# A decoder layer whose input norm moves behind the first matmuls

## The chip, the core and the metric

The kernel runs on one core of a Trainium2 chip. The core has a matmul engine (PE, with its weight loads PEld), three engines for elementwise work (DVE, ACT, POOL), a queue engine (SP) that issues most transfers, and 16 DMA engines. The metric is the device time of one execution in microseconds (us). The kernel before takes 607.66 us, the median of three runs that lie between 607.46 and 608.18.

## The reference, cut to what matters

One layer of a hybrid decoder on 1024 tokens of 1024 features, in float32. `D = S = 1024`; there are four heads of differential attention (group A) and four of chunkwise retention (group B), each with 128 columns of values.

```python
u = rmsnorm(h, norm_pre_w)                     # h * rsqrt(mean(h*h) + eps) * w, per token
proj = einsum('bsd,de->bse', u, w_in)          # 1024 x 1024 @ 1024 x 4096
dq, dk, dv, dg, rq, rk, rv, rg = split(proj)   # 512 columns each
lam = exp(sum(q1*k1)) - exp(sum(q2*k2)) + lambda_init
# group A: rotary on dq, dk; p_c = softmax(causal(q_c k_c^T / 8)), c = 0, 1; (p_0 - lam * p_1) @ dv
y_a = rmsnorm(diff_attention(dq, dk, dv, positions, lam), diff_subln_w) * (1 - lambda_init)
y_a = y_a * silu(dg)
# group B: rotary on rq, rk; scores decayed by g^(i-j), g = 1 - 2^-(5+head), times rv
y_b = rmsnorm(retention_chunkwise(rq, rk, rv, positions)) * silu(rg)
y = concatenate([y_a, y_b]) @ w_out
return h + rmsnorm(y, norm_post_w)
```

The factor 1/rms of the first line belongs to one token, so it is the same for all of a token's features. A projection of the unnormalised token, times that factor, is the projection of the normalised one.

## The kernel before

**Tiles.** Tokens stand in `NT = 8` tiles of 128, features in `KT = 8` tiles of 128. `u` is held transposed (features on the partitions), in halves of 512 tokens, each as two parts that add up to the float32 value: `uh` (rounded to the format that the matmul multiplies) and `ul` (the rest). `w_in` comes as 16 packed blocks of 256 columns, in the order of `ORDER`: part 0 of a head holds its values and gates, part 1 its queries and keys. A block is loaded in four chunks (`load_chunk`, L147), each rounded by ACT into `whi` and completed by DVE or POOL in turn into `wlo` (`split_lo`, L141; two of four turns each). A product is three matmuls: `uh*whi + uh*wlo + ul*whi` (L296 to L298 for outputs with tokens on the partitions, L308 to L310 for transposed outputs).

**The beginning.** For each token tile, `norm_tile` (L257) squares x on ACT with a running sum, takes `(mean + eps) ** -0.5` with DVE and POOL (`rsqrt`, L132), multiplies x by it and by the gain on DVE (L272), transposes the eight 128x128 pieces on PE into two PSUM banks (L278), and splits them into `uh` (ACT, L281) and `ul` (DVE, L282). After every second tile, `main_group(0, ...)` multiplies two token tiles by block 0 (`proj_rows`, L285) into one of two PSUM banks named `pj`. Then come the angles of the rotary embedding (`angles`, L174: a long chain on DVE, two sines on ACT, 16 transposes on PE at L229) and the rest of the blocks.

**The rest.** `main_group(b, g)` is a quarter of a block. What the quarter yields is read from PSUM by `values_gates` (L313: values by ACT at L321 or L325, `tanh` of the gate by ACT at L327, `gt = (tanh + 1) * gate` by DVE at L328), by `diff_qk` (L354, with the rotary factors `cosD`, `sinD`) or by `ret_qk` (L458, with `cosE`, `sinE`). Between the quarters stand pieces of other heads' attention and retention. The last block's quarters are followed by the output projection.

**What sets the order.** The program is written once, in one stream. A scheduler then puts each engine's instructions in a fixed order by its own estimate of when each can run; so PE's queue interleaves pieces that stand apart in the code, and SP's queue holds loads ahead of those that the code writes first. On the chip each engine takes its queue strictly in that order.

Of the kernel before, what the change touches and what calls it, by code (L numbers as in the profile page):

```python
# [10 lines left out]
F32 = mybir.dt.float32  # L11
# [20 lines left out]
# Column layout of the constants that depend on shapes alone.  # L32
# [8 lines left out]
# Heads (differential 0-3, retention 4-7) and the order of their blocks of w_in:  # L41
# part 0 holds the values and gates, part 1 the queries and keys.
# [46 lines left out]
def body(ctx, tc, x, pos, wpk, wout, vecs, npre, npost, subln, cst, out):  # L89
# [32 lines left out]
    cs = const.tile([P, NCST], F32, name="cs")  # L122
# [6 lines left out]
    halves = const.tile([P, 2], F32, name="halves")  # L129
    nc.gpsimd.memset(halves, -0.5)  # L130

    def rsqrt(dst, src, more):  # L132
        """(src + more) ** -0.5"""
# [7 lines left out]
    def split_lo(dst, full, hi):  # L141
        """dst = full - hi, rounded to the tensor engine's operand (exact)."""
# [31 lines left out]
    def angles(tp, posi):  # L174
        """cos and sin of position * frequency, with an exact reduction to one turn."""
# [29 lines left out]
        # small parts first  # L205
# [8 lines left out]
        # cos x = sin(x + a quarter turn)  # L214
# [32 lines left out]
    def load_x(xin, t):  # L247
        xt = xin.tile([P, D], F32, tag="xt", name="xt")
        rows = slice(t * P, (t + 1) * P)
        if t == 0:  # L250
            nc.sync.dma_start(xt[:, 0:512], x[rows, 0:512])
            nc.scalar.dma_start(xt[:, 512:], x[rows, 512:])
        else:
            nc.sync.dma_start(xt, x[rows, :])
        return xt

    def norm_tile(xp, t, xt, npw):  # L257
        xu = xp.tile([P, D], F32, tag="xu", name="xu")
        ms = xp.tile([P, 2], F32, tag="ms", name="ms")
        rs = xp.tile([P, 1], F32, tag="rs", name="rs")  # L260
        if t == 0:
            for i in range(2):
                sl = slice(i * 512, (i + 1) * 512)
                nc.scalar.activation(xu[:, sl], xt[:, sl], AF.Square, scale=1.0 / math.sqrt(D),
                                     accum_out=ms[:, i:i + 1])
            nc.vector.tensor_scalar(ms[:, 0:1], ms[:, 0:1], EPS, None, op0=ALU.add)
            rsqrt(rs, ms[:, 1:2], ms[:, 0:1])
        else:
            nc.scalar.activation(xu, xt, AF.Square, scale=1.0 / math.sqrt(D), accum_out=ms[:, 0:1])
            rsqrt(rs, ms[:, 0:1], EPS)  # L270
        for sl in (slice(0, 512), slice(512, D)) if t == 0 else (slice(0, D),):
            nc.vector.scalar_tensor_tensor(xu[:, sl], xt[:, sl], rs, npw[:, sl], op0=ALU.mult, op1=ALU.mult)  # L272
        cols = slice(t % 4 * P, (t % 4 + 1) * P)
        for g in range(2):
            ps = pm()
            for q in range(4):
                kt = g * 4 + q
                nc.tensor.transpose(ps[:, q * P:(q + 1) * P], xu[:, kt * P:(kt + 1) * P], ident)  # L278
            pv = ps.rearrange("p (k c) -> p k c", k=4)
            hs = uh[t // 4][:, g * 4:(g + 1) * 4, cols]  # L280
            nc.scalar.copy(hs, pv)  # L281
            nc.vector.tensor_tensor(ul[t // 4][:, g * 4:(g + 1) * 4, cols], pv, hs.bitcast(F32),  # L282
                                    op=ALU.subtract)
# [17 lines left out]
    def proj_cols(w, f, half):  # L301
        """128 features of the block over 512 tokens, transposed."""
# [10 lines left out]
    def values_gates(st, w, t2):  # L313
        if t2 == 0:
# [3 lines left out]
        ps = proj_rows(w, t2)  # L318
        sl = slice(2 * t2, 2 * t2 + 2)
        if st["h"] < H:  # L320
            nc.scalar.copy(v[:, sl, :], ps[:, :, 0:P])  # L321
        else:
            for j in range(2):
                c = C_VSC + (st["h"] - H) * NT + 2 * t2 + j
                nc.scalar.activation(v[:, 2 * t2 + j, :], ps[:, j, 0:P], AF.Copy, scale=cs[:, c:c + 1])  # L325
        th = rp.tile([P, 2, P], F32, tag="th", name="th")
        nc.scalar.activation(th, ps[:, :, P:2 * P], AF.Tanh, scale=0.5)  # L327
        nc.vector.scalar_tensor_tensor(gt[:, sl, :], th, 1.0, ps[:, :, P:2 * P],  # L328
# [5 lines left out]
    def emit_y(st, t, o_ps, tot):  # L334
        """The head's output, normalised and gated, to its columns of y."""
# [18 lines left out]
    def diff_qk(st, w, g):  # L354
        """Step g of 4: features (first, second rotary halves) of each half of the tokens."""
# [31 lines left out]
    def diff_scores(st, i):  # L387
# [4 lines left out]
        for u in range(2):  # L392
            nm = sm_.tile([P, 2], F32, tag="nm", name="nm")
            banks = []
            for b, (k0, kn) in enumerate(pieces):
# [5 lines left out]
                if last:  # L401
                    # -(scores with the mask), and the least of it
# [33 lines left out]
    def diff_values(st, i):  # L436
# [21 lines left out]
    def ret_qk(st, w, t2):  # L458
        ps = proj_rows(w, t2)
# [14 lines left out]
    def ret_chunks(st, t2):  # L474
# [58 lines left out]
    def split_wout(nh, ms):  # L533
        """Rows of w_out for half nh of the columns, scaled by what y was not yet scaled by."""
# [238 lines left out]
```

## Time and profile before

| quantity | value |
|---|---|
| median of three runs | 607.66 us |
| span of the profiled execution | 606.4 us |
| PE busy | 588.3 us (97%) |
| DVE busy | 324.4 us (53%) |
| ACT busy | 236.1 us (39%) |
| POOL busy | 140.7 us (23%) |
| bytes moved | 59.66 MB in 36196 packets |

The span runs from the first to the last instruction of one profiled execution. The page gives no other time of that execution; the median of the runs is 1.26 us longer than the span, and this is taken as what lies around it. "Busy" counts an engine's instructions, so an engine can be busy and slow. The end of a matmul is modelled; the distance between the starts of two matmuls tells their rate.

### The profile page before, as it was taken

The page shows a single profiled execution, that of the slowest core. Times are in us where ns is not written, and L with a number is a line of the kernel's source. Part 1 is how long each engine was busy: PE and PEld are TensorE (multiplying, and loading weights), DVE is VectorE, ACT ScalarE, POOL GpSimd, SP SyncE. Part 2 cuts the span into 40 slices and gives each one's busy share as a digit, 9 for nine tenths or more (in the row PEclk, how much of TensorE's full clock was granted, in tenths as well). Part 3 has the DMA queues.
Part 4 walks back from the last instruction along what each step waited for, and adds up shares of the span by engine and source line. Part 5 has one row for each costly group of instructions (what it writes and reads, how often), then busy time and mean ns, then how long its engine had stood idle before and what let it go on. Part 6 is the DMA issues. An engine that isn't in the chain of part 4 may idle for free.

```text
span 606.4 us, 10873 instructions
## 1 busy us (share of the span) xinstructions
PE 588.3 (97%) x4144; PEld 552.3 (91%) x4144; DVE 324.4 (53%) x820; ACT 236.1 (39%) x652; POOL 140.7 (23%) x171
## 2 busy tenths in 40 slices
PE   4999999999999999999999999999999999999995
PEld 3999989999989999999899998899999988888884
DVE  4888335755654357723444556456566673343232
ACT  5643522444433343534134445223546443212110
POOL 4303124411224032313241102343310230000000
PEclk9999999999999999999999999999999999999999
DMA  8602237510228420202185202482202372332221
GB/s 298 237 2 71 70 69 174 161 33 22 76 59 224 92 80 9 79 10 78 37 189 152 79 10 78 92 222 66 67 27 79 112 272 62 122 119 76 91 69 71
DMA packets 36196, 59.66 MB, mean 98 GB/s; under 512 B 4784, under 2 KB 12208, under 8 KB 36144
## 3 DMA queue, kind: packets, MB, share of 16 engines
q1 hardware_dynamic: 36000, 58.70, 33.0%
q8 instruction: 33, 0.54, 0.3%
q10 hardware_dynamic: 144, 0.26, 0.1%
q14 instruction: 19, 0.16, 0.1%
HBM read 34.30 MB, written 7.86 MB: 70 GB/s over the span
## 4 chain that ended last, share of the span: by engine, by line
PE 95%; DVE 1%; DMA 1%; issue 1%; ACT 0%; POOL 0%; SPq 0%; DVEq 0%; POOLq 0%; ACTq 0%
PE pj L296 15%; PE pj L298 15%; PE pj L297 15%; PE sc L399 6%; PE pm L449 5%; PE pj L308 5%; PE pj L310 5%; PE pj L309 5%; PE pm L444 3%; PE pj L585 2%; PE op L585 2%; PE pj L587 2%; PE pj L586 2%; PE op L587 2%; PE op L586 2%; PE pm L566 1%
## 5 line engine op out<-in xcount | busy, mean ns | idle before, releaser
L296 PE MATMUL pj<-whi,uh 128*128 128x256 f32 x768 | 221.6, 289 | 1.0 <-ACT uh L281 1.0
L298 PE MATMUL pj<-whi,ul 128*128 128x256 f32 x768 | 221.1, 288 | 0.5 <-DVE ul L282 0.5
L297 PE MATMUL pj<-wlo,uh 128*128 128x256 f32 x768 | 219.9, 286 | 0.0
L296 PEld LDWEIGHTS pj<-whi,uh 128*128 128x128 f32 x768 | 148.1, 193 | 2.1 <-ACT uh L281 1.6
L298 PEld LDWEIGHTS pj<-whi,ul 128*128 128x128 f32 x768 | 148.0, 193 | 1.0 <-DVE ul L282 0.8
L297 PEld LDWEIGHTS pj<-wlo,uh 128*128 128x128 f32 x768 | 148.1, 193 | 0.6
L135 POOL TENSOR_TENSOR tot<-tot,halves 128x1 f32<-128x1 f32 (+1 forms) x56 | 34.5, 616 | 275.3 <-DVE tot L134 273.2
L413 ACT ACTIVATE p<-sc,nm 128x384 f32<-128x384 f32 (+5 forms) x96 | 55.1, 580 | 53.8 <-DVE nm L403 52.5
L145 POOL TENSOR_TENSOR wlo<-raw,whi 128x512 fp32r<-128x512 f32 x32 | 46.4, 1453 | 78.5 <-ACT whi L152 68.8
L152 ACT CAST whi<-raw 128x512 fp32r<-128x512 f32 x64 | 39.4, 623 | 34.3 <-PE pj L309 17.5
L308 PE MATMUL pj<-uh,whi 128*128 128x512 f32 x128 | 50.5, 394 | 0.0
L309 PE MATMUL pj<-ul,whi 128*128 128x512 f32 x128 | 50.4, 394 | 0.0
L310 PE MATMUL pj<-uh,wlo 128*128 128x512 f32 x128 | 50.2, 392 | 0.0
L399 PE MATMUL sc<-ks,qs 128*128 128x384 f32 (+5 forms) x192 | 46.1, 346 | 0.0
L449 PE MATMUL pm<-v,at 128*128 128x128 f32 x288 | 39.7, 275 | 0.0
L447 ACT COPY at<-pm 128x512 f32<-128x512 f32 (+3 forms) x48 | 23.1, 481 | 42.4 <-PE pm L444 42.3
L449 PEld LDWEIGHTS pm<-v,at 128*128 128x128 f32 x288 | 36.8, 192 | 0.6
L145 DVE TENSOR_TENSOR wlo<-raw,whi 128x512 fp32r<-128x512 f32 x32 | 26.1, 827 | 19.9 <-ACT whi L152 19.0
L343 DVE SCALAR_TENSOR_TENSOR y<-pm,tot,gt 128x128 f32<-128x128 f32 x56 | 18.4, 348 | 24.9 <-POOL tot L135 16.6
L399 PEld LDWEIGHTS sc<-ks,qs 128*128 128x128 f32 x192 | 30.5, 191 | 1.0
L403 DVE CUSTOM_DVE_ANT_0 sc<-sc,mask,nm 128x320 f32<-128x320 f32 (+3 forms) x32 | 21.0, 655 | 18.8 <-PE sc L399 18.6
L434 ACT ACTIVATE sq<-pm,cs 128x128 f32<-128x128 f32 x32 | 11.4, 363 | 47.5 <-PE pm L511 47.4
(145 smaller groups left out, 971.5 us busy)
## 6 DMA issues: line engine op xcount, KB each, us to landing
raw<-in_wpk SPq DMA_DIRECT2D x64, 256.0 KB, 3.4
xt<-in_x SPq DMA_DIRECT2D x15, 512.0 KB, 3.8
ks<-rhi SPq DMA_DIRECT2D x32, 128.0 KB, 2.4
qs<-rhi SPq DMA_DIRECT2D x32, 128.0 KB, 2.4
ks<-rlo SPq DMA_DIRECT2D x32, 128.0 KB, 2.4
qs<-rlo SPq DMA_DIRECT2D x32, 128.0 KB, 2.4
raw<-in_wout SPq DMA_DIRECT2D x16, 256.0 KB, 3.0
out<-ob SPq DMA_DIRECT2D x16, 256.0 KB, 2.4
```

What stands on the lines that cost most here:

```text
L135: nc.gpsimd.tensor_tensor(dst, dst, halves[:, 0:dst.shape[-1]], op=ALU.pow)
L145: eng.tensor_tensor(dst, full, hi.bitcast(F32), op=ALU.subtract)
L152: nc.scalar.copy(hi, raw)
L296: nc.tensor.matmul(dst, lhsT=a, rhs=wh, start=(kt == 0 and j == 0), stop=False)
L297: nc.tensor.matmul(dst, lhsT=a, rhs=wl, start=False, stop=False)
L298: nc.tensor.matmul(dst, lhsT=b, rhs=wh, start=False, stop=(kt == KT - 1 and j == 1))
L308: nc.tensor.matmul(ps, lhsT=wh, rhs=uh[half][:, kt, :], start=(kt == 0), stop=False)
L309: nc.tensor.matmul(ps, lhsT=wh, rhs=ul[half][:, kt, :], start=False, stop=False)
L310: nc.tensor.matmul(ps, lhsT=wl, rhs=uh[half][:, kt, :], start=False, stop=(kt == KT - 1))
L399: nc.tensor.matmul(sp[:, 0:kn], lhsT=st["q"][:, u, r, i * P:(i + 1) * P], rhs=st["k"][:, u, r, k0:k0 + kn], start=(r == 0), stop=(r == 1))
L413: nc.scalar.activation(p[:, k0:k0 + kn], banks[b][:, 0:kn], AF.Exp, scale=-1.0 if b == np_ - 1 else 1.0, bias=nm[:, np_ - 1:np_], accum_ou ...
L449: nc.tensor.matmul(o_ps[:, 0:P], lhsT=at[:, j * P:(j + 1) * P], rhs=v[:, j0 + j, :], start=(j0 + j == 0), stop=(j0 + j == i))
```

## The change

The host gives x a second time, transposed (`xt_in`). `load_u` loads two feature tiles of 512 tokens, multiplies by the gain of the feature (now one number per partition) and splits at once into `uh` and `ul`; nothing is divided by the rms, and nothing is transposed on PE. `mean_squares` loads x by token tiles and squares them on ACT; 1/rms of all tokens stands in `rs`, half of it in `rsh`. It is multiplied into the outputs: into the values when they leave PSUM, into the argument of `tanh`, into the normalising factor of each head's output (for the gate), and into `cosE` and `sinE` (for queries and keys, and through them `cosD` and `sinD`). The first block is multiplied with the feature tile as its outermost loop, over four PSUM banks: two `pj` for the first half of the tokens, two `pm` for the second. The banks are read after `rs` is there.

```diff
@@ angles
             nc.scalar.activation(eo, v, AF.Sin, scale=scale)
+            nc.vector.tensor_tensor(eo, eo, rs.unsqueeze(2).broadcast_to([P, NT, 64]), op=ALU.mult)
@@ load_x, norm_tile
-    def norm_tile(xp, t, xt, npw):
...
+    def load_u(xin, half, k0, kn):
+        xk = xin.tile([P, 2, HT], F32, tag="xk", name="xk")
+        nc.sync.dma_start(xk[:, 0:kn, :], xt_in[:, k0:k0 + kn, half * HT:(half + 1) * HT])
+        for j in range(kn):
+            kt = k0 + j
+            hs, sc = uh[half][:, kt, :], npw[:, kt:kt + 1]
+            nc.scalar.activation(hs, xk[:, j, :], AF.Copy, scale=sc)
+            nc.vector.scalar_tensor_tensor(ul[half][:, kt, :], xk[:, j, :], sc, hs.bitcast(F32),
+                                           op0=ALU.mult, op1=ALU.subtract)
+
+    def mean_squares(xp, ms, t):
+        xr = xp.tile([P, D], F32, tag="xr", name="xr")
+        nc.sync.dma_start(xr, x[t * P:(t + 1) * P, :])
+        sq = xp.tile([P, D], F32, tag="xsq", name="xsq", bufs=1)
+        nc.scalar.activation(sq, xr, AF.Square, scale=1.0 / math.sqrt(D), accum_out=ms[:, t:t + 1])
+
+    def proj_rows(w, t2s, banks):
+        for kt in range(KT):
+            wh, wl = weight(w, kt)
+            for t2, ps in zip(t2s, banks):
+                for j in range(2):
...
@@ values_gates
-            nc.scalar.copy(v[:, sl, :], ps[:, :, 0:P])
...
-        nc.scalar.activation(th, ps[:, :, P:2 * P], AF.Tanh, scale=0.5)
...
+        for j in range(2):
+            t = 2 * t2 + j
+            sc = rs[:, t:t + 1] if st["h"] < H else vsc[:, st["h"] - H, t:t + 1]
+            nc.scalar.activation(v[:, t, :], ps[:, j, 0:P], AF.Copy, scale=sc)
+            nc.scalar.activation(th[:, j, :], ps[:, j, P:2 * P], AF.Tanh, scale=rsh[:, t:t + 1])
@@ diff_values
         rsqrt(tot, ms, e1)
+        nc.gpsimd.tensor_tensor(tot, tot, rs[:, i:i + 1], op=ALU.mult)
@@ the program
+        first = proj_rows(w0, [0, 1], [pj(), pj()])
+        for c in range(4):
+            load_u(xin, 1, 2 * c, 2)
+        second = proj_rows(w0, [2, 3], [pm(), pm()])
...
+        blocks[1] = load_block(1)
+        ms = tp.tile([P, NT], F32, name="xms")
+        for t in range(NT):
+            mean_squares(xp, ms, t)
+            if t % 4 == 3:
+                rsqrt(rs[:, t - 3:t + 1], ms[:, t - 3:t + 1], EPS)
+        nc.vector.tensor_scalar(rsh, rs, 0.5, None, op0=ALU.mult)
...
+        for t2, ps in enumerate(first + second):
+            values_gates(heads[0], w0, t2, ps)
...
+        angles(tp, posi, cs)
```

In the orders below a row is the line in the code (of the kernel it belongs to), the operation, output<-inputs, the shape, and how many stand in a row.

ACT's queue around the two sines of the angles, in the kernel before (`v`, `th` are values and gates of a finished projection, `whi` a weight chunk):

```order
L325 ACTIVATE v<-pj,cs 128x128 x2
L327 ACTIVATE th<-pj 128x256
L220 ACT_TABLE_LOAD
L220 ACTIVATE sinE<-acc 128x512
L220 ACTIVATE cosE<-t_608 128x512
L325 ACTIVATE v<-pj,cs 128x128 x2
L327 ACT_TABLE_LOAD
```

The same place in the changed kernel (`xsq` is the square of a token tile of x; the last of the eight stands here):

```order
L152 CAST whi<-raw 128x512
L269 ACTIVATE xsq,xms<-xr 128x1024
L226 ACT_TABLE_LOAD
L226 ACTIVATE sinE<-acc 128x512
L269 ACTIVATE xsq,xms<-xr 128x1024
L152 CAST whi<-raw 128x512
L226 ACTIVATE cosE<-t_524 128x512
L326 ACTIVATE v<-pm,rs 128x128 x2
L327 ACT_TABLE_LOAD
L327 ACTIVATE th<-pj,rsh 128x128
```

The eighth square, and with it 1/rms of the second half of the tokens, stands behind the first sine, which reads the end of the angle chain on DVE; before, the squares were done long before the angles.

DVE's queue at the end of the angle chain, in the kernel before (`acc` and `t` carry the angles, `A`, `B`, `C` are copies of the cosines and sines for PE's transposes, `gt` is the gate):

```order
L193 TENSOR_TENSOR acc<-acc,t_609 128x512
L215 TENSOR_SCALAR t_608<-acc 128x512
L328 SCALAR_TENSOR_TENSOR gt<-th,pj 128x256
L189 TENSOR_SCALAR t_609<-t_608 128x512
L226 COPY C<-sinE 128x4x32 x4
L193 TENSOR_TENSOR t_608<-t_608,t_609 128x512
L226 COPY t_609<-sinE 128x4x32 x4
L226 COPY A<-cosE 128x4x32 x4
```

The same place in the changed kernel:

```order
L199 TENSOR_TENSOR acc<-acc,t_525 128x512
L221 TENSOR_SCALAR t_524<-acc 128x512
L195 TENSOR_SCALAR t_525<-t_524 128x512
L199 TENSOR_TENSOR t_524<-t_524,t_525 128x512
L134 TENSOR_SCALAR rs<-xms 128x4
L648 TENSOR_SCALAR rsh<-rs 128x8
L651 TENSOR_TENSOR vsc<-cs,rs 128x32
L651 TENSOR_TENSOR osc<-cs,rs 128x32
L227 TENSOR_TENSOR cosE<-cosE,rs 128x512
L227 TENSOR_TENSOR sinE<-sinE,rs 128x512
L233 COPY A<-cosE 128x4x32 x4
L233 COPY B<-cosE 128x4x32 x2
```

The next row there is the first `gt`, the one that frees the first `pj` bank. In the kernel before, the four gates of the first block and two of the second's had been made by this place; now the first one of all follows the whole angle chain.

## Rows read from the trace of the kernel before

**Rows 1.** The page, chain that ended last: share of the span by engine

```profile
PE 95%; DVE 1%; DMA 1%; issue 1%; ACT 0%; POOL 0%; SPq 0%; DVEq 0%; POOLq 0%; ACTq 0%
```

**Rows 2.** Windows: stretch and length, busy us per engine (instructions), PE clock, DMA share, GB/s

```profile
100.00:200.00 100.00, 100.00 (x741) 95.44 (x740) 58.26 (x163) 41.65 (x127) 29.16 (x35) 1.00 0.38 101
```

**Rows 3.** Waits of PE: for whom, total us, times, longest

```profile
PE pm L278 <- DVE xu L272: 8.0, 2, 7.1
```

**Rows 4.** Timeline of PE: start, us, line, operation, shape, count

```profile
11.86 0.42 PE L296 MATMUL pj<-whi,uh 128*128 128x256 f32 x1
...
16.12 0.42 PE L298 MATMUL pj<-whi,ul 128*128 128x256 f32 x1
...
24.05 0.28 PE L298 MATMUL pj<-whi,ul 128*128 128x256 f32 x1
...
29.08 0.28 PE L298 MATMUL pj<-whi,ul 128*128 128x256 f32 x1
...
69.59 0.40 PE L308 MATMUL pj<-uh,whi 128*128 128x512 f32 x1
```

**Rows 5.** The chain in order of time: transposes of the angles, start and us

```profile
64.13 0.88 PE pm L229 x8
```

**Rows 6.** Windows (columns as in rows 2) at the kernel's end

```profile
599.00:600.00 1.00, 0.50 (x3) 0.08 (x1) 0.00 (x0) 0.40 (x1) 0.00 (x0) 1.00 0.00 0
...
604.00:605.00 1.00, 0.00 (x0) 0.00 (x0) 0.00 (x0) 0.00 (x0) 0.00 (x0) 0.82 0.86 326
```

**Rows 7.** Windows (columns as in rows 2) while the first loads run

```profile
11.00:12.00 1.00, 0.52 (x2) 0.52 (x3) 1.00 (x3) 1.00 (x3) 0.00 (x0) 1.00 1.06 432
...
21.00:22.00 1.00, 1.00 (x11) 1.00 (x10) 1.00 (x2) 1.00 (x3) 0.25 (x1) 1.00 0.99 373
```

**Rows 8.** Timeline of ACT (columns as in rows 4; in brackets the wait before)

```profile
4.08 0.63 ACT L264 ACTIVATE xu<-xt 128x512 f32<-128x512 f32 x1 [1.56 <-DMA xt<-in_x]
...
10.46 1.07 ACT L269 ACTIVATE xu<-xt 128x1024 f32<-128x1024 f32 x1
...
58.74 0.63 ACT L220 ACTIVATE sinE<-acc 128x512 f32<-128x512 f32 x1
...
62.93 1.28 ACT L327 ACT_TABLE_LOAD   x1
```

**Rows 9.** Lines L545 and L546: ns min/median/max, first and last start, shape

```profile
L545 ACT ACTIVATE woh<-raw,wos x8: 707/719/740, 461.3 to 481.6; 128x512 fp32r<-128x512 f32 x8
...
L546 DVE SCALAR_TENSOR_TENSOR wol<-raw,wos,woh x8: 739/747/1237, 462.1 to 484.2; 128x512 fp32r<-128x512 f32 x8
```

**Rows 10.** Timeline of DVE (columns as in rows 4)

```profile
13.30 2.30 DVE L272 SCALAR_TENSOR_TENSOR xu<-xt,rs,npw 128x1024 f32<-128x1024 f32 x1 [0.45 <-POOL rs L135]
...
20.79 1.28 DVE L272 SCALAR_TENSOR_TENSOR xu<-xt,rs,npw 128x1024 f32<-128x1024 f32 x1
...
39.68 0.41 DVE L328 SCALAR_TENSOR_TENSOR gt<-th,pj 128x256 f32<-128x256 f32 x1
...
42.02 0.42 DVE L189 TENSOR_SCALAR A<-ang 128x512 f32<-128x512 f32 x1
42.48 0.69 DVE L202 TENSOR_TENSOR C<-ang,A 128x512 f32<-128x512 f32 x1
...
46.23 1.29 DVE L145 TENSOR_TENSOR wlo<-raw,whi 128x512 fp32r<-128x512 f32 x2
...
48.37 1.19 DVE L209 TENSOR_SCALAR t<-A 128x512 f32<-128x512 f32 x1
...
61.34 0.63 DVE L226 COPY A<-cosE 128x128 f32<-128x128 f32 x4
```

**Rows 11.** Timeline of POOL (columns as in rows 4)

```profile
13.24 1.28 POOL L145 TENSOR_TENSOR wlo<-raw,whi 128x512 fp32r<-128x512 f32 x1
...
20.08 0.55 POOL L135 TENSOR_TENSOR rs<-rs,halves 128x1 f32<-128x1 f32 x1 [2.48 <-DVE rs L134]
...
45.15 5.55 POOL L145 TENSOR_TENSOR wlo<-raw,whi 128x512 fp32r<-128x512 f32 x2 [9.34 <-PE pj L298]
```

More of the change, by code (lines that the diff above doesn't have):

```diff
@@ L86, in two_pi_parts, with body @@
     return a1, a2, a3, b1, b2, float(inv)
-def body(ctx, tc, x, pos, wpk, wout, vecs, npre, npost, subln, cst, out):
+def body(ctx, tc, x, xt_in, pos, wpk, wout, vecs, npre, npost, subln, cst, out):
     nc = tc.nc
@@ L119, in g2k @@
         return gen.tile([P, 512], F32, tag="g", name=name)
-    cs = const.tile([P, NCST], F32, name="cs")
+    rsc = const.tile([P, H * NT], F32, name="rsc")
     ident = const.tile([P, P], F32, name="ident")
@@ L127, in body @@
     sub = const.tile([P, 1], F32, name="sub")
-    halves = const.tile([P, 2], F32, name="halves")
+    halves = const.tile([P, NT], F32, name="halves")
     nc.gpsimd.memset(halves, -0.5)
@@ L166, in body @@
     ul = [upool.tile([P, KT, HT], F32R, tag=f"ul{i}", name=f"ul{i}") for i in range(2)]
+    rs = const.tile([P, NT], F32, name="rs")
+    rsh = const.tile([P, NT], F32, name="rsh")
+    vsc = const.tile([P, H, NT], F32, name="vsc")
+    osc = const.tile([P, H, NT], F32, name="osc")
+    npw = const.tile([P, KT], F32, name="npw")
     cosE = const.tile([P, NT, 64], F32, name="cosE")
@@ L172, in body, with angles @@
     nlam = const.tile([P, 1], F32, name="nlam")
-    def angles(tp, posi):
+    def angles(tp, posi, cs):
         a1, a2, a3, b1, b2, inv = two_pi_parts()
@@ L245, in lambdas @@
         nc.vector.tensor_scalar(nlam, nlam, -LAM_INIT, None, op0=ALU.add)
[L247 to L255, printed above, removed]
-    def norm_tile(xp, t, xt, npw):
[L258 to L283, printed above, removed]
@@ new lines, in mean_squares @@
+    def mean_squares(xp, ms, t):
[9 more added lines that the diff above has]
+                    t = 2 * t2 + j
+                    dst = ps[:, j * 256:(j + 1) * 256]
+                    cols = slice(t % 4 * P, (t % 4 + 1) * P)
+                    a = uh[t // 4][:, kt, cols]
+                    b = ul[t // 4][:, kt, cols]
+                    nc.tensor.matmul(dst, lhsT=a, rhs=wh, start=(kt == 0 and j == 0), stop=False)
+                    nc.tensor.matmul(dst, lhsT=a, rhs=wl, start=False, stop=False)
+                    nc.tensor.matmul(dst, lhsT=b, rhs=wh, start=False, stop=(kt == KT - 1 and j == 1))
+        return [ps.rearrange("p (j f) -> p j f", j=2) for ps in banks]
@@ L311, in proj_cols, with values_gates @@
         return ps
-    def values_gates(st, w, t2):
-        if t2 == 0:
+    def values_gates(st, w, t2, ps=None):
+        if "v" not in st:
             st["v"] = vgp.tile([P, NT, P], F32, tag="v", name="v")
@@ L606, in main_group @@
         st = heads[n]
-        if g == (0 if b else 2) and b + 1 < NB:
+        if g == 0 and b + 1 < NB:
             blocks[b + 1] = load_block(b + 1)
@@ L617, in main_group @@
             blocks.pop(b)
-    with tc.tile_pool(name="xin", bufs=4) as xin, tc.tile_pool(name="xp", bufs=2) as xp, tc.tile_pool(name="tp", bufs=1) as tp:
-        npw = tp.tile([P, D], F32, name="npw")
-        xts = {0: load_x(xin, 0)}
-        nc.sync.dma_start(npw, npre.partition_broadcast(P))
-        norm_tile(xp, 0, xts.pop(0), npw)
-        blocks[0] = [load_chunk(0, c, xin) for c in range(2)]
-        xts[1] = load_x(xin, 1)
-        blocks[0] += [load_chunk(0, c, xin) for c in range(2, 4)]
-        xts[2], xts[3] = load_x(xin, 2), load_x(xin, 3)
-        for t in range(NT):
-            if t:
-                norm_tile(xp, t, xts.pop(t), npw)
-            if t + 4 < NT:
-                xts[t + 4] = load_x(xin, t + 4)
-            if t % 2:
-                main_group(0, t // 2)
+    with tc.tile_pool(name="xin", bufs=4) as xin, tc.tile_pool(name="xp", bufs=4) as xp, tc.tile_pool(name="tp", bufs=1) as tp:
+        nc.scalar.dma_start(npw, npre)
+        w0 = []
+        for c in range(4):
+            if c == 0:
+                load_u(xin, 0, 0, 1)
+                w0.append(load_chunk(0, c))
+                load_u(xin, 0, 1, 1)
+            else:
+                w0.append(load_chunk(0, c))
+                load_u(xin, 0, 2 * c, 2)
+        blocks[0] = w0
+        first = proj_rows(w0, [0, 1], [pj(), pj()])
+        for c in range(4):
+            load_u(xin, 1, 2 * c, 2)
+        second = proj_rows(w0, [2, 3], [pm(), pm()])
+        cs = tp.tile([P, NCST], F32, name="cs")
@@ L639, in body @@
+        nc.vector.tensor_scalar(rsh, rs, 0.5, None, op0=ALU.mult)
+        rsb = rs.unsqueeze(1).broadcast_to([P, H, NT])
+        for dst, c in ((vsc, C_VSC), (osc, C_OSC)):
+            nc.vector.tensor_tensor(dst, cs[:, c:c + H * NT].rearrange("p (h t) -> p h t", h=H), rsb, op=ALU.mult)
+        for t2, ps in enumerate(first + second):
+            values_gates(heads[0], w0, t2, ps)
+        blocks.pop(0)
         nc.vector.tensor_scalar(wo["s"], sub, 0.5 * (1.0 - LAM_INIT), None, op0=ALU.mult)
@@ L645, in body @@
                                 pattern=[[1, P]], channel_multiplier=-1)
-        angles(tp, posi)
+        angles(tp, posi, cs)
         lambdas(tp)
```

33 lines of the change are left out of this document (15 added, 18 removed).

## The prediction

> **What bounds the kernel now.** I read the chain that ended last first: 95% of the span is PE [rows 1]. The windows then show where PE has slack: from 100 to 200 us it is busy for 100.00 of 100 us [rows 2]. So a faster DVE or ACT gains nothing there, and what the change can win or lose lies where PE stands idle or does work that the result doesn't need: the beginning. The waits of PE show 8.0 us before the transposes of `xu` at L278, 7.1 of it in one piece at the start [rows 3]. The timeline of PE gives two paces. From 11.86 to 16.12 us lie 20 matmuls of 256 columns, 0.213 us apart; from 24.05 to 29.08 lie 42, 0.1198 apart [rows 4]. These are 256 columns at about 1.2 and 2.4 GHz. A block is 192 such matmuls, 23.0 us at the fast pace. The mark that I compare at is the first matmul of block 2 (L308): 69.59 us [rows 4]. Before it PE has made blocks 0 and 1 (46.0 us) and 16 transposes of the angles; the other 22 us are the late start, 64 transposes of u, the slow pace, and short waits. Behind it PE's order changes only by pieces shifted against each other, so the sum is made at this mark.
>
> **What the change removes.** 64 transposes of u, at 0.11 us each (0.88 for eight [rows 5]), are 7.0 us of PE. The first matmul now needs one feature tile of x and one chunk of weights, and no rms. Neither counts by itself, since PE is to wait for something else before block 1.
>
> **What it adds: one long wait.** All four banks of block 0 are read only after `rs`. The first quarter of block 1 needs a `pj` bank, and PE's order has the four transposes of `A` (copies of `cosE` times `rs`) right behind block 0. Both wait for the end of the angle chain on DVE: ACT's order holds the first sine, which reads that chain, ahead of the eighth square. So I add up DVE's queue.
>
> *Its start.* The first 0.52 MB of x is in use at 4.08 us [rows 8]. Loads then run at 373 to 432 GB/s [rows 7]; at 400, the rest of 2.1 MB of transposed x (first half) and 1.05 MB of weights takes 6.5 us, to 10.6. Two splits on ACT (0.72 each) and one on DVE (0.75) [rows 9] end at 12.8. Until there DVE waits for data; from there its queue has always something ready: the next data come at 400 GB/s, ahead of it.
>
> *Its length.* From there to the end of the chain (`acc`) the order holds 8 splits of x at 0.75 [rows 9], 15 operations of two tensors at 0.69 (11 of the angles, 4 of weights), 10 of one tensor at 0.42 [rows 10], and 14 short ones, an estimate of 0.24 each, under the 0.42 of a wide one. Together 6.0 + 10.4 + 4.2 + 3.3 = 23.9 us. Operations overlap at their ends: the nine from 42.02 to 46.23, five of 0.42 and four of 0.69, take 4.21 us where their durations add up to 4.86, 0.87 of it [rows 10]. I take 0.9, since part of the list needs the operation just before: 21.5 us.
>
> *Its neighbour.* While POOL ran a split of weights from 13.24 [rows 11], DVE's L272 took 2.30 us instead of 1.28; and in the stretch of two such splits, 45.15 to 50.70 [rows 11], L209 took 1.19 instead of the 0.42 of such an operation [rows 10]. So a split on POOL costs DVE 0.8 to 1.0 us, and nothing where DVE waits anyway. Three of them (both of block 1 and one of block 2) and one power (0.55 [rows 11]) fall into the list: between 0 and 4.4 us, I take 3 x 0.9 + 0.5 = 3.2, near the rows.
>
> The chain on DVE ends at 12.8 + 21.5 + 3.2 = 37.5 us. ACT and the loads are there before: the 33 loads up to the eighth tile of x are 11.5 MB, so the last lands near 32 us.
>
> *The tail.* Sine 0.63, square 1.07 [rows 8], reading of the sum and four handovers (an estimate: 0.6), the addition 0.15, the power 0.55 [rows 11]: 3.0 us. A split of weights on POOL follows the power at once and costs DVE 0.9 more. Then three short products (0.6), `cosE` and `sinE` times `rs` (2 x 0.69), four copies (0.63) and two (0.3), the first `gt` (0.41) [rows 10], overlapped 2.4 us. The `tanh` table (1.28 [rows 8]) and ACT's other work end before. The first matmul of block 1 starts at 37.5 + 3.0 + 0.9 + 0.6 + 2.4 + 0.1 = 44.5 us.
>
> *PE's side.* The last split of the second half is 10 rows before the chain's end, near 31 us, so block 0 is done by about 33 us and PE stands idle for some 10 us. At the kernel's end the last matmul is over at 599.5, and the granted clock falls within 604 to 605 [rows 6]. So 5 idle us were enough there, and block 1 starts at the slow pace. A slow matmul costs 0.093 us more. At the start of the kernel before, PE was slow from the first work after its 7.1 us wait until past 16 us [rows 3, 4]: 28 to 36 matmuls, 2.6 to 3.4 us. Here it may be nothing (if the clock holds) to 3.4; I take 2.4, close under that row, because four transposes run ahead.
>
> *Sum.* 44.5 + 23.0 (block 1) + 1.5 (the other 12 transposes, 0.11 each, with the changes of shape) + 2.4 = 71.4 us at the mark, against 69.59: 1.8 us later. The span goes from 606.4 to 608.2; with the 1.26 us around it, by which the median stands over the span, 609.5 us.
>
> **A rule that weighs more.** In the stretch at 13.24 POOL took its usual 1.28 us and DVE lost 1.02 [rows 10, 11]. The Trainium skill ("SBUF — State Buffer", section "SBUF: two separate sides") says why: DVE with two inputs from SBUF and POOL share a pair of ports as an exclusive lock, and the loser is blocked for the whole instruction. The row bears that out. By the rule alone the change, which turns the splits of u from PSUM inputs into SBUF inputs, puts 16 more operations under the lock.
>
> **Costs that I put at nothing.** The second reading of x (4.2 MB) lands 5 us before its last square's turn. `values_gates` now has four ACT instructions for three or two, 0.6 us more per quarter of 5.7 us; ACT is busy 41.65 of 100 us [rows 2], and two `pj` banks cover it. The product with `rs` on POOL lengthens the way to the output of each of 32 attention tiles by one small operation, 0.55 us like the power [rows 11]; PE, never idle in rows 2, hides it as far as the three `pm` banks reach. If that cover were gone everywhere, it would be 32 x 0.55 = 17.6 us.
>
> **The rivals.**
> *Not slower: POOL slips into gaps.* DVE's list has handovers in which POOL can run, and at 46.23 two splits of DVE took 1.29 together, undisturbed, beside POOL's 5.55 [rows 10, 11]; there POOL waited, not DVE. With nothing lost in the list the chain ends at 34.3, the tail is 6.1 long, block 1 starts at 40.4. With a short slow phase (1.6) the mark is at 66.5: 3.1 us gained, 604.6 us. It decides when the chain ends before 34.5: then the gain passes 1.2 us even with the usual slow phase. Against it: two of the three cases show DVE losing. 0.20.
> *No difference.* The chain ends between 34.5 and 36.9, as when half of the price is paid: the mark moves by less than 1.2 us, 607.7 us. 0.27.
> *The lock in full.* Each split costs DVE the whole 1.28 (four of them, 1.5 us more) and the power its 0.55: 611.1 us, and 612.1 with the slow phase at 3.4. Against it: the row's 1.02 is below it. The rule of the Trainium skill named above would have it so. 0.15.
> *The product on POOL holds the banks.* PE waits at a few of the 32 tiles: 1 to 5 us on top, 610 to 614 us. Against it: the power stands in the same chain today, and PE is never idle in rows 2. 0.05.
> *The banks don't hold PE back,* and the 7.0 us of transposes are won: 600 us. The order excludes it, since the first `gt` follows the whole chain. 0.01, within the 0.20.
>
> **How the numbers follow.** The forecast itself, which holds 608.9 to 611, has 0.33; slower in all 0.33 + 0.15 + 0.05 = 0.53. About 0.2%, 1.2 us, is what a measurement can tell here from no change. Same 0.27, faster 0.20. The range runs from the first rival's 604.6 to the lock in full with the long slow phase, near 612.3. The cases of a loss alone would be 608.9 to 612.3.
>
> **What would show it.** Right: one wait of PE of 9 to 12 us at the transposes of `A` and then at L298, ended by DVE; the sine starting near 37 us, the eighth square right behind it; matmuls 0.21 us apart after 44 us; L308 first at about 71. Wrong in the chain's length: the sine before 35. Wrong in the clock: a pace of 0.12 from the first matmul of block 1. Wrong in the whole: PE idle between 100 and 500 us, or no wait before block 1.

## The result, and the profile after

| | before | after |
|---|---|---|
| median, us (four runs each, same chip) | 607.62 (607.46 to 608.18) | 612.20 (611.25 to 612.53) |
| span of the profiled execution, us | 606.4 | 610.8 |
| first matmul of block 2 (the mark), us | 69.59 [rows 4] | 73.21 |
| PE busy from 100 to 500 us | 398.57 | 400.00 |

The change makes the kernel slower: the ratio of the times is 1.0068, with a 95% interval from 1.0054 to 1.0082. The forecast was 609.5, in a range from 604.6 to 612.3.

The span grew by 4.4 us, and 3.6 of them stand ahead of the mark. First the waits of PE, in the columns of [rows 3]:

```profile
PE pm L236 <- DVE A L233: 9.7, 1, 9.7
PE pj L282 <- ACT whi L152: 6.3, 1, 6.3
PE pm L284 <- DVE ul L262: 2.3, 3, 1.6
PE pm L488 <- ACT qkT L485: 1.0, 1, 1.0
```

The first wait for data (6.3) is a little shorter than the 7.1 us of [rows 3]; the one behind block 0 (9.7) is new. The windows (columns as in [rows 2]) show what it does to the clock, and that the middle of the kernel lost nothing:

```profile
30.00:40.00 10.00, 4.46 (x33) 3.84 (x32) 9.90 (x20) 7.72 (x16) 3.85 (x3) 1.00 0.68 261
40.00:50.00 10.00, 3.85 (x18) 3.85 (x19) 7.85 (x29) 8.56 (x21) 2.25 (x2) 0.55 0.15 55
50.00:60.00 10.00, 10.00 (x82) 10.00 (x81) 0.42 (x1) 2.99 (x7) 0.00 (x0) 0.94 0.00 0
...
100.00:500.00 400.00, 400.00 (x3039) 385.57 (x3038) 224.58 (x614) 176.34 (x533) 109.61 (x153) 1.00 0.34 93
```

PE's timeline around the wait (columns as in [rows 4]) shows the end of block 0, the first transposes, the first matmul of block 1, the last slow ones and the first fast ones:

```profile
36.16 0.28 PE L284 MATMUL pm<-whi,ul 128*128 128x256 f32 x1
46.15 1.12 PE L236 MATMUL pm<-ident,A 128*128 128x128 f32 x4 [9.71 <-DVE A L233]
46.92 0.56 PE L298 MATMUL pj<-whi,uh 128*128 128x256 f32 x1
...
50.90 0.41 PE L298 MATMUL pj<-whi,uh 128*128 128x256 f32 x1
51.12 0.34 PE L299 MATMUL pj<-wlo,uh 128*128 128x256 f32 x1
51.29 0.28 PE L300 MATMUL pj<-whi,ul 128*128 128x256 f32 x1
```

Block 0 is done at 36.4 us. Then PE stands idle for 9.7 us, and the first 20 matmuls of block 1 run at the slow pace.

Behind the mark lie the other 0.8 us. There the kernel after has waits of 1.0, 0.8 and 0.3 at L488, L567 and L513, and the kernel before has 0.6 and 0.8 in the same two places (its L486 and L566): 0.7 us more.

### The profile page after: what moved, and what is told of

It is laid out like the page before. It is cut to its first block, busy times and chain, and to the rows that moved or that the text cites. A ratio compares the mean times of both kernels' runs of the same rounds, so it can differ in the third digit from the quotient of the medians.

```text
span 610.8 us, 10801 instructions
## 1 busy us (share of the span) xinstructions
PE 582.9 (95%) x4080; PEld 546.8 (90%) x4080; DVE 317.1 (52%) x809; ACT 250.0 (41%) x698; POOL 142.2 (23%) x197
## 4 chain that ended last, share of the span: by engine, by line
PE 90%; DVE 5%; DMA 2%; ACT 1%; issue 1%; POOL 1%; DVEq 0%; POOLq 0%; ACTq 0%
PE pj L298 14%; PE pj L299 14%; PE pj L300 14%; PE sc L400 6%; PE pm L450 5%; PE pj L311 5%; PE pj L312 5%; PE pj L310 5%; PE pm L445 3%; PE pj L588 2%; PE pj L586 2%; PE op L588 2%; PE op L587 2%; PE op L586 2%; PE pj L587 2%; DMA xk<-in_xt 2%
## 5 line engine op out<-in xcount | busy, mean ns | idle before, releaser
L298 PE MATMUL pj<-whi,uh 128*128 128x256 f32 x704 | 202.9, 288 | 0.0
L300 PE MATMUL pj<-whi,ul 128*128 128x256 f32 x704 | 201.7, 286 | 0.0
L299 PE MATMUL pj<-wlo,uh 128*128 128x256 f32 x704 | 201.3, 286 | 0.0
L299 PEld LDWEIGHTS pj<-wlo,uh 128*128 128x128 f32 x704 | 135.5, 193 | 0.5
L298 PEld LDWEIGHTS pj<-whi,uh 128*128 128x128 f32 x704 | 135.5, 192 | 0.5
L300 PEld LDWEIGHTS pj<-whi,ul 128*128 128x128 f32 x704 | 135.4, 192 | 0.2
L145 POOL TENSOR_TENSOR wlo<-raw,whi 128x512 fp32r<-128x512 f32 x32 | 43.0, 1344 | 106.3 <-ACT whi L152 77.0
L145 DVE TENSOR_TENSOR wlo<-raw,whi 128x512 fp32r<-128x512 f32 x32 | 26.3, 831 | 17.9 <-ACT whi L152 16.3
L312 PEld LDWEIGHTS pj<-uh,wlo 128*128 128x128 f32 x128 | 24.1, 188 | 4.8
```

Of the source, the lines that this page charges most:

```text
L145: eng.tensor_tensor(dst, full, hi.bitcast(F32), op=ALU.subtract)
L298: nc.tensor.matmul(dst, lhsT=a, rhs=wh, start=(kt == 0 and j == 0), stop=False)
L299: nc.tensor.matmul(dst, lhsT=a, rhs=wl, start=False, stop=False)
L300: nc.tensor.matmul(dst, lhsT=b, rhs=wh, start=False, stop=(kt == KT - 1 and j == 1))
L312: nc.tensor.matmul(ps, lhsT=wl, rhs=uh[half][:, kt, :], start=False, stop=(kt == KT - 1))
```

## The experiments

Each starts from the changed kernel. The first theory was the prediction's: block 0's results hold their banks until the angle chain on DVE is done, and block 1 waits for a bank. The times of the experiments, with the kernel before run on the same chip:

| run | time, us | ratio to before (95%) | mark, us |
|---|---|---|---|
| after | 612.20 | 1.0068 (1.0054 to 1.0082) | 73.21 |
| a_banks | 602.97 | 0.9917 (0.9889 to 0.9946) | 64.36 |
| b_angles_late | 608.88 | 1.0018 (1.0009 to 1.0028) | 67.40 |
| c_both | 601.01 | 0.9897 (0.9876 to 0.9919) | 57.20 |
| h_sine_late | 612.20 | 1.0071 (1.0056 to 1.0086) | 72.67 |
| d3 | 611.73 | 1.0065 (1.0052 to 1.0077) | 71.86 |
| e_warm | 609.92 | 1.0031 (1.0019 to 1.0042) | 70.95 |
| f_layout | 612.61 | 1.0068 (1.0054 to 1.0082) | 73.34 |
| i_halves | 602.40 | 0.9912 (0.9899 to 0.9926) | 61.88 |
| k_late_halves | 600.77 | 0.9894 (0.9877 to 0.9911) | 57.46 |
| o_late3 | 600.22 | 0.9875 (0.9861 to 0.9888) | 58.36 |
| n_g3 | 599.68 | 0.9870 (0.9856 to 0.9883) | 58.03 |

With late angles (b, c, k, o and n) the 16 transposes of the angles, some 1.8 us, come behind the mark.

**a_banks: block 0 in other banks.**

```diff
-first = proj_rows(w0, [0, 1], [pj(), pj()])
-second = proj_rows(w0, [2, 3], [pm(), pm()])
+first = proj_rows(w0, [0, 1], [psc(), psc()])   # banks of the scores, idle until then
+second = proj_rows(w0, [2, 3], [psc(), pm()])
```

> Block 0's four groups of features go into the three banks of the scores and one of pm, so that both banks of pj are free while block 0's gates are still to come. In the changed kernel TensorE stands still from 36.4 to 46.1 us, and the slow clock and short waits behind it bring the first matmul of block 2 to 73.4. Theory (block 0's results hold the banks, and block 1 waits for the gates that free them behind the chain of the angles): block 1 starts in the free banks, the wait of 9.7 shrinks to under 2, TensorE does block 1's rows while VectorE does the angles, the first matmul of block 2 comes at 61 to 64 and the time falls by 9 to 12 us, to 600 to 603. Rival 1 (the loads set block 0's end and what follows): with the banks free nothing changes, 611 to 612. Rival 2 (VectorE is behind as a whole, so that the wait only moves to where block 1's outputs want their gates): the wait of 9.7 goes but one of over 5 turns up before 75 us, and the time falls by under 5, to 607 to 611.

The long wait is gone and the time falls by 9.2 us (1.5%). The median is in the theory's range and the mark nearly (64.36 for 61 to 64); both rivals are out. The four runs lie apart: two took 604.12 us (this trace) and 604.79, at a mean granted clock of 0.990 and 0.992, and two took 601.62 and 601.82, at 0.997 and 0.996. What is left, in PE's timeline:

```profile
46.19 0.66 PE L239 MATMUL pm<-ident,A 128*128 128x128 f32 x4 [1.22 <-DVE A L236]
...
48.54 1.12 PE L239 MATMUL pm<-ident,C 128*128 128x128 f32 x4 [0.82 <-ACT cosD L241]
...
51.13 0.58 PE L301 MATMUL pj<-whi,uh 128*128 128x256 f32 x1 [0.62 <-DVE gt L332]
```

So held banks are what turns late gates into a wait. Why the gates are late is another question, and there the theory did worse:

**b_angles_late: the angles behind block 0's gates.**

```diff
 nc.vector.tensor_copy(posf, posi)
+nc.vector.tensor_scalar(zero, heads[0]["g"][:, NT - 1, 0:1], 0.0, None, op0=ALU.mult)
+nc.vector.tensor_scalar(posf, posf, zero, None, op0=ALU.add)
```

> The positions' cast waits for a gate of block 0 (zero times one of its values is added), so that the whole chain of the angles on VectorE comes behind block 0's gates instead of ahead of them. Theory (VectorE's list of 23.5 us of angles stands ahead of the first gate): the first gate comes at about 20 to 38 us instead of 46.3, TensorE's wait between block 0 and block 1 falls from 9.7 to under 2, the first matmul of block 2 comes at 61 to 64, and the time is 599 to 603. Rival 1 (the loads set it): no change, 611 to 612. Rival 2 (the angles are needed right behind block 0 anyway, by the turned outputs of block 1): the wait only moves behind block 1, 607 to 612.

All three were wrong. The time falls by 3.3 us only; that is in the range of rival 2, but the wait didn't move behind block 1: PE still waits 7.7 us between block 0 and block 1. The chain in order of time, of this run, tells for what (start, us, engine, line):

```profile
29.40 8.21 DMA xr<-in_x
...
37.69 0.61 ACT xsq L272
...
39.39 0.76 POOL rs L135
...
40.17 1.23 DVE rsh L651
...
41.43 0.37 ACT th L330
...
42.34 0.43 DVE gt L332
...
42.91 0.55 PE pj L301
```

With the angles out of the way, the first gate waits for the eighth tile of x, read a second time, its square, and 1/rms. But the first gate belongs to the first quarter of the tokens, and the squares of the whole first half were done by 29.4 us in this run. It waits because `rsh` (half of 1/rms, the scale inside `tanh`) is one operation over all eight tiles. So two chains of different length end at one gate: the angles' at 46.3, the mean squares' at 42.3.

**c_both: the two together.**

> Both edits together: block 0 in the banks of the scores and one of pm, and the angles behind block 0's gates. Theory: each of the two alone already takes away the wait of 9.7 and with it the slow clock behind it, so that both together give no more than the better one alone by over 1.5 us: 598 to 602. Rival (the two causes are two halves of the wait, each worth about 5): the sum of the two, with each alone at 606 to 608 and both at 600 to 602.

601.01 is in the theory's range, but 2.0 us below the better one alone, where it had at most 1.5. That miss is no finding: against the two runs of a_banks whose granted clock was as high, the difference is 0.7. The rival is out: a alone is worth 9.2 of the 11.2 us, so the edits are not two halves of one wait. PE's waits from 10 to 100 us are 1.7 for a gate and 1.2 for `m` (L373), where the late angles now arrive late for block 2.

**h_sine_late: the eighth square no longer behind the sine.**

```diff
-nc.scalar.activation(eo, v, AF.Sin, scale=scale)
+nc.scalar.activation(eo, v, AF.Sin, bias=zero, scale=scale)   # zero = 0 * rs
```

> The two sines take as bias zero times 1/rms, so they come behind the last square on ScalarE and not ahead of it, and 1/rms, with it the gates, need not wait for the chain of the angles. Theory: block 0's gates go ahead of the turn of the angles; the wait of 9.7 shrinks by what VectorE's and ScalarE's order gives back, to 2 to 6, and the slow clock behind it by up to 1.9; time 603 to 608. Rival (the chain of the angles occupies VectorE until 39.9 whatever ScalarE's order is, and the gates stand behind it): the wait stays at 8 to 10, and the time at 610 to 612.

The theory missed and the rival came true, within 0.2 us: 612.2, and a wait of 9.0. The wait now stands at block 1's first matmul itself, with the transposes of `A` behind it, so it isn't the place of the transposes in PE's order that makes it:

```profile
PE pj L300 <- DVE gt L331: 9.0, 1, 9.0
```

ACT finished the eighth square 2.6 us sooner (its sum read at 38.78 instead of 41.41), but on DVE the next step stood in line. DVE's timeline:

```profile
41.12 0.69 DVE L199 TENSOR_TENSOR t<-t,t 128x512 f32<-128x512 f32 x1
41.73 0.16 DVE L134 TENSOR_SCALAR rs<-xms 128x4 f32<-128x4 f32 x1
43.02 1.22 DVE L650 TENSOR_SCALAR rsh<-rs 128x8 f32<-128x8 f32 x1 [1.13 <-POOL rs L135]
```

`rs` follows the last operation of the angles, as it did in the changed kernel (41.63). So the order of ACT, which the prediction gave as the reason, can go and nothing is won: DVE's order holds the gate at the same place. The reverse was not tried. In the changed kernel the two orders end together, the angles on DVE at 41.54 and the sum of the eighth square on ACT at 41.60 (DVE first, then ACT):

```profile
40.85 0.69 DVE L199 TENSOR_TENSOR t<-t,t 128x512 f32<-128x512 f32 x1
41.63 0.17 DVE L134 TENSOR_SCALAR rs<-xms 128x4 f32<-128x4 f32 x1
```

```profile
41.41 0.19 ACT L269 ACTIVATION_READ_ACCUMULATOR xsq<-xr 128x1 f32 x1
```

**d3: two of POOL's splits on DVE.** Only the choice of the engine is changed, for two weight splits of block 2.

```diff
-eng = nc.vector if lo_turn[0] % 4 in (2, 3) else nc.gpsimd
+eng = nc.vector if lo_turn[0] % 4 in (2, 3) or lo_turn[0] in (9, 12) else nc.gpsimd
```

> The two splits of weights for block 2 that GpSimd did (it worked until 34.6 and from 42.9 to 44.1) go to VectorE. The order around the angles' turn stays the same. Theory (VectorE is held while GpSimd's split runs: the row of 1.79 us at 33.4 and the one of 1.22 at 42.9 are instructions that take 0.65 and 0.1 to 0.2 elsewhere; a split costs VectorE 0.65 itself): the end of the chain comes 0 to 1 us earlier, and the first gate 0.5 to 2 us earlier, the time falls by 0.3 to 2, to 610 to 612. Rival 1 (the lock is the whole of what made the kernel slower): it falls by 4 or more, to under 608. Rival 2 (GpSimd's work beside VectorE costs it nothing): the two splits make VectorE's list longer by 1.3, and the time rises by 1 to 2, to 613 to 614.

The time moved by 0.5 us, and the two intervals overlap, so it doesn't separate the theory from no effect. It speaks against rival 2, but hardly against rival 1: by the rows below the two splits on POOL cost DVE 2.1 us, and on DVE they cost it some 1.4 (two of 0.68), so a fall of 4 could not have come of this edit, whatever the lock is worth in all. The trace is clearer: span 609.8 for 610.8, mark 71.86 for 73.21, and the same instructions have their plain durations. DVE in this run:

```profile
33.49 0.74 DVE L262 SCALAR_TENSOR_TENSOR ul<-xk,npw,uh 128x512 fp32r<-128x512 f32 x1
...
42.53 0.17 DVE L648 TENSOR_SCALAR rsh<-rs 128x8 f32<-128x8 f32 x1
```

and in the changed kernel, first DVE, then POOL beside it:

```profile
29.27 1.52 DVE L195 TENSOR_SCALAR t<-t 128x512 f32<-128x512 f32 x1
...
33.38 1.79 DVE L262 SCALAR_TENSOR_TENSOR ul<-xk,npw,uh 128x512 fp32r<-128x512 f32 x1
...
42.94 1.22 DVE L648 TENSOR_SCALAR rsh<-rs 128x8 f32<-128x8 f32 x1 [1.13 <-POOL rs L135]
```

```profile
28.82 1.69 POOL L145 TENSOR_TENSOR wlo<-raw,whi 128x512 fp32r<-128x512 f32 x1 [9.99 <-ACT whi L152]
...
32.68 1.94 POOL L145 TENSOR_TENSOR wlo<-raw,whi 128x512 fp32r<-128x512 f32 x1
...
42.87 1.26 POOL L145 TENSOR_TENSOR wlo<-raw,whi 128x512 fp32r<-128x512 f32 x1
```

Each split on POOL costs DVE 1.05 to 1.1 us (1.79 against 0.74, 1.22 against 0.17, 1.52 against the 0.42 of such an operation). The rule in the prediction names instructions of DVE with two inputs; L195 and L648 have one and are held as long. Two of POOL's own splits are stretched too (1.69 and 1.94, the others 1.26 to 1.40).

**e_warm: PE kept at work through the wait.** 64 matmuls of 256 columns, read by nobody, behind block 0.

```diff
+dummy = ps_s.tile([P, 512], F32, tag="sc", name="sc")
+wh0, _ = weight(w0, KT - 1)
+for n in range(64):
+    nc.tensor.matmul(dummy[:, 0:256], lhsT=ul[1][:, KT - 1, 384:512], rhs=wh0, start=True, stop=True)
```

> 64 matmuls of 256 columns whose results nobody reads go behind block 0, so that TensorE does not stand still for all of the 9.7 us ahead of block 1. Theory: in the changed kernel TensorE's granted clock is 0.55 in the slice from 40 to 50 us, and some 20 matmuls of block 1 take 0.213 instead of 0.12 us, 1.9 us in all; here the granted clock stays high or nearly so, the first matmul of block 2 comes at about 71.5 to 72.5 instead of 73.4, and the time falls by 1 to 2, to 610 to 611.5. Rival 1 (the time lost is the wait alone and the slow matmuls are made up for later): no change, 611.5 to 612.5. Rival 2 (the added matmuls delay what TensorE has to do, the angles' transposes): slower by 1 or more, over 613.

2.3 us faster, a little more than the theory had, and both rivals are out. Windows of 40 to 50 us and PE's timeline of this run:

```profile
40.00:50.00 10.00, 8.43 (x70) 8.02 (x69) 7.12 (x30) 8.49 (x21) 2.58 (x2) 1.00 0.09 28
```

```profile
36.49 7.84 PE L639 MATMUL sc<-whi,ul 128*128 128x256 f32 x64
45.32 0.66 PE L236 MATMUL pm<-ident,A 128*128 128x128 f32 x4 [0.99 <-DVE A L233]
46.56 0.36 PE L298 MATMUL pj<-whi,uh 128*128 128x256 f32 x1 [0.58 <-DVE gt L329]
```

Block 1 starts 0.36 us earlier than in the changed kernel (46.92), and the mark is 2.26 earlier: some 1.9 us of it are the granted clock, 1.00 here and 0.55 there, as the 20 slow matmuls at 0.093 us each had it.

**f_layout: longer runs of bytes in x's loads.** The host packs transposed x by halves of the tokens.

```diff
-nc.sync.dma_start(xk[:, 0:kn, :], xt_in[:, k0:k0 + kn, half * HT:(half + 1) * HT])
+nc.sync.dma_start(xk[:, 0:kn, :], xt_in[:, half, k0:k0 + kn, :])
```

> x lies in the array on the device by halves of its rows, so that each partition's piece of a load of two features is one run of bytes twice as long as before. Theory (the loads of the first 10 us are slow because they start when the queues and the weights' loads start, as they do in the kernel before the change): the last pair of the first half is squared at 13.98 us or at most 0.7 earlier, and the time changes by under 1, 611 to 612.5. Rival (short runs of bytes slow them): the last pair lands at 10.5 to 12.5, VectorE's list starts 1.5 to 3.5 earlier, and the time falls by 1.5 to 4, to 608 to 610.5.

No change (612.61); the last pair of the first half is at ACT at 13.85 instead of 13.98. The rival is out.

**i_halves: rsh by halves, nothing else.** This follows from b.

```diff
 if t % 4 == 3:
     rsqrt(rs[:, t - 3:t + 1], ms[:, t - 3:t + 1], EPS)
-nc.vector.tensor_scalar(rsh, rs, 0.5, None, op0=ALU.mult)
+    nc.vector.tensor_scalar(rsh[:, t - 3:t + 1], rs[:, t - 3:t + 1], 0.5, None, op0=ALU.mult)
```

> Half of 1/rms (rsh, the scale inside the gates' tanh) is worked out for each half of the rows by itself, and not for all eight tiles at once behind the last square. Nothing else is changed: same banks, same angles. What the runs so far left: with the angles behind the gates the first gate still came at 42.34 us, in a chain of eighth square to 38.84, rs to 40.14, rsh (1.22) and tanh. Theory (the gates of the first half, whose bank block 1 wants first, wait for the mean squares of the second half, which are read from x a second time as the last of the loads): the first gate comes at 34 to 38 us instead of 46.3, TensorE's wait of 9.7 falls to under 2, the clock does not fall, the first matmul of block 2 comes at 61 to 63.5, and the time is 600 to 602.5. Rival 1 (the chain of the angles holds the gates by itself, as it stands ahead of them on VectorE): the wait stays over 5, the time at 607 to 611. Rival 2 (the wait moves to block 1's turned outputs, which need the angles): the first gate comes early, but a wait of over 3 turns up between 45 and 75 us, 603 to 607.

602.40: 9.8 us faster than the changed kernel and 0.9% faster than before, from one small operation made in two pieces. The edit is that one operation; the new places of the gates on DVE, and of the transposes of `A` on PE (now from 47.73), are the scheduler's answer to it. DVE's timeline shows the first gate amid the angles; the last operation below is the end of their list:

```profile
33.97 0.15 DVE L648 TENSOR_SCALAR rsh<-rs 128x4 f32<-128x4 f32 x1
...
35.71 0.40 DVE L329 SCALAR_TENSOR_TENSOR gt<-th,pj 128x256 f32<-128x256 f32 x1
...
40.40 0.69 DVE L199 TENSOR_TENSOR t<-t,t 128x512 f32<-128x512 f32 x1
```

and PE waits for it 0.95 us, in place of 9.7:

```profile
36.26 0.36 PE L298 MATMUL pj<-whi,uh 128*128 128x256 f32 x1 [0.95 <-DVE gt L329]
```

Rival 1, that the angles hold the gates by themselves because they stand ahead of them on DVE, is out: with `rsh` of the first half made by itself, at 34 us, the first two gates stand amid them. No wait of rival 2's kind appeared. What is left of ACT's order shows in the second half of the tokens, where `rs` waits for the eighth square behind the sine; it holds only gates that PE hardly waits for (0.56 us):

```profile
42.61 0.17 DVE L134 TENSOR_SCALAR rs<-xms 128x4 f32<-128x4 f32 x1 [1.52 <-ACT xsq L269]
```

POOL has its splits as before (DVE's L262 takes 1.78 us beside one of them), so rival 1 of d3 is out as well: the loss goes while the lock stays.

**k_late_halves, o_late3, n_g3: with the angles later as well.** k is b and i together. o lets the angles wait for a gate of the first half (`NT // 2 - 1` for `NT - 1` in b's edit). n is o with a's banks.

> rsh by halves, and the angles behind all of block 0's gates. Theory (two chains end at the first gate, the angles' at 46.3 and the mean squares' at 42.3, and taking away one leaves the other): here neither is left, the wait of 7.7 that stayed with the angles late alone falls to under 2, and the time falls from 608.9 to 600 to 602.5. Rival (it is neither, the loads of x and of the weights hold block 1's start): 607 to 609.

> rsh by halves, and the angles wait for a gate of the first half only, so that they run while the second half's gates are still to come. Theory: no wait over 1.5 in the first 75 us, 599.5 to 602, as fast as the version with other banks and late angles (601.0). Rival (the last gates now stand behind part of the angles and hold the banks of pm, which the turn of the angles wants): a wait of 2 to 5 at those transposes, 603 to 606.

> The same as the one before (rsh by halves, angles behind the first half's gates), with block 0 in three banks of the scores and one of pm besides. Theory (with rsh by halves no bank is missing any more): within 1.5 of the version without other banks, 599 to 601.5. Rival (the banks are worth something of their own, as they were with late angles: 601.0 against 608.9): faster by 2 or more than that version.

All three theories held, at 600.77, 600.22 and 599.68. k settles b: the 7.7 us that b left vanish with the split of `rsh`, so it was the second chain. o's only wait of PE over 0.6 us from 10 to 75 us is one of 1.2 for a gate. n's banks add 0.5 us to o, about what can't be told from nothing: here the banks mattered only while the gates were late. n has the lowest time, 1.3% below the kernel before, and isn't told apart from o.

## Why the prediction was right in its sign, and what was wrong in it

The forecast of 609.5 was 2.7 us short, and the loss is 4.6 us where 1.9 was forecast. 612.20 lies above the forecast's own case (608.9 to 611), 0.1 under the end of the range, and where "the lock in full" was put, which is not the reason. That it lies in the range at all is owed to the width.

*The place* held: one wait of 9.7 us (forecast 9 to 12) at the transposes of `A`, the sine right before the eighth square, slow matmuls behind it, and nothing between 100 and 500 us. Of the rivals, "the banks don't hold PE back" got its meaning from a_banks: with the banks free the kernel takes 603.0, near the 600 put for it (607.66 less 7.0 is 600.7).

*The mis-sized term* is the start of DVE's unbroken list, 12.8 in the forecast and 16.4 in the trace. ACT's timeline of the changed kernel shows the last pair of the first half in use at 13.98, where 10.6 was put:

```profile
3.73 1.28 ACT L261 ACT_TABLE_LOAD   x1 [3.73 <-DMA xk<-in_xt]
...
13.98 1.34 ACT L261 ACTIVATE uh<-xk,npw 128x512 fp32r<-128x512 f32 x2 [0.22 <-DMA xk<-in_xt]
```

The rate of 400 GB/s came from [rows 7], at 11 and 21 us. The first microseconds run slower, as windows of the changed kernel show:

```profile
5.00:6.00 1.00, 0.00 (x0) 0.00 (x0) 0.22 (x1) 0.99 (x3) 0.00 (x0) 1.00 0.85 199
6.00:7.00 1.00, 0.69 (x2) 0.50 (x2) 0.62 (x2) 0.88 (x2) 0.66 (x1) 1.00 0.78 233
7.00:8.00 1.00, 0.39 (x2) 0.28 (x2) 1.00 (x1) 0.00 (x0) 0.67 (x1) 1.00 1.06 389
```

SP's own timeline has a gap there: eight loads go out by 4.8 us, and the next one waits until 6.56.

```profile
4.12 0.67 SPq L150 DMA_DIRECT2D raw<-in_wpk  x1
6.56 0.38 SPq L257 DMA_DIRECT2D xk<-in_xt  x1
```

SP's wait is for `ul` (L262): a buffer of x comes free when DVE has split it. The load that waits is the last pair itself: the first half comes in five loads, and `xin` has four buffers. The chain of this run (start, us, what) goes through it:

```profile
6.56 7.40 DMA xk<-in_xt
```

The forecast let the loads run without a stop, so it missed this gap of 1.8 us. How much of the 3.4 us the gap makes, and how much the low rate, was not tried; f_layout shows that the length of the runs isn't the reason.

*The list itself* was too long by 1.2 us, lock and all: 23.5 us (16.4 to 39.9) for 24.7. The lock took about what was put there for three splits on POOL, 0.9 each: two cost 1.1 and 1.05 (the rows under d3), and beside the one at 17.5 us six narrow operations of the angles took 2.13, where two took 0.42 just before. So the chain's end was 39.9 for 37.5, 3.6 late and 1.2 back.

*The tail* (7.0 us from the chain to block 1's first matmul, forecast 7.0, partly by luck: the power took 1.02 where 0.55 was put, and what stands ahead of it was 0.5 shorter), *the slow clock* (1.9 for 2.4) and *PE's side* (26.3 us from that matmul to the mark, for 26.9) were near. At the mark the forecast was short by 1.8 us (73.21 for 71.4), behind the mark by 0.8, and the time exceeds the span by 1.4 us for 1.26. (The profiled execution of the changed kernel took 612.53 us, 1.7 over its own span, and the listed runs of both kernels lie 1.7 to 1.8 over theirs; 1.26 and 1.4 set the span of one execution against the median of several.)

*The step that failed without showing in the number* is the reason that was given for the late gate: "Both wait for the end of the angle chain on DVE: ACT's order holds the first sine, which reads that chain, ahead of the eighth square." The order is as told, but h_sine_late shows that without it the gate is hardly earlier (45.19 for 46.29), and i_halves that the gates of the first half needed neither the angles nor the eighth square. What bound them was the operand `rsh` over all tokens. The diff has it in one line; the prediction asked only when the last of `rs` is there. In the same way "The second reading of x (4.2 MB) lands 5 us before its last square's turn", put at nothing, held only behind a longer chain: in b_angles_late, where that is gone, the last load goes out at 29.40 and lands at 37.61, where near 32 was put, and it ends the chain that PE waits for.

*The rule on the lock* agrees with the trace in its mechanism (the rows under d3: DVE loses 1.05 to 1.1 us beside a split of 1.3 to 1.9), and the sum took it at about the size the rows gave. At some 1 us for each of four splits it lengthens the wait, but it isn't what makes it: i_halves has the same splits and no long wait.

## What to carry to other kernels

Where a result holds a buffer until a late operand is there, list the operand's inputs tile by tile: a small operation that is done once over all tiles makes the first tile wait for the last, and here splitting it in two was worth 9.8 us of 612. When two chains end at one wait, taking away the longer shows only the difference (3.3 us in b), so look for what the shorter one is before pricing the fix. And take the rate of the first loads from the first microseconds of the trace, not from its steady part, and count the buffers that they go into.

## What the runs showed of the hardware that was not expected

A granted clock can fall without one long pause: in the trace of a_banks it fell with waits of 1.22, 0.22, 0.82 and 0.62 us between the transposes of the angles, from 45 to 51 us. The windows of that run:

```profile
40.00:50.00 10.00, 7.73 (x57) 7.06 (x56) 7.59 (x29) 9.69 (x26) 2.28 (x2) 0.90 0.15 53
50.00:60.00 10.00, 9.38 (x63) 8.98 (x62) 1.17 (x4) 3.70 (x12) 0.00 (x0) 0.76 0.01 2
```

The matmuls behind them ran at 0.213 us, the pace at 1.2 GHz, until 54.5. It doesn't always fall so: two of that kernel's four runs had a mean clock of 0.996 and 0.997, and what was different in them no trace shows. One wait with matmuls on both sides of it left the clock at 1.00, 1.16 us long in o_late3 and 1.69 in c_both.

ACT's table load can lie on the way or beside it. In the changed kernel the first one starts only when the first piece of x has landed (3.73 above), and its 1.28 us lie on the way to the first matmul at 6.31; in the kernel before it starts at 1.24, ahead of the data. The one for the sine doesn't wait for the sine's input:

```profile
37.53 1.28 ACT L226 ACT_TABLE_LOAD   x1
39.93 0.63 ACT L226 ACTIVATE sinE<-acc 128x512 f32<-128x512 f32 x1 [1.12 <-DVE acc L199]
```
